# Tokens of the experts: an indirect DMA of rows and transposes on TensorE, where products with one-hot places stood

## The chip, the cores and the metric

The kernel runs on one core of a Trainium2 chip. The metric is the device time of one execution in microseconds (us). The engines are named as in the profile: PE (TensorE), DVE (VectorE), ACT (ScalarE), POOL (GpSimd), SP (SyncE, which here only issues transfers), and the 16 DMA engines of the core. Weights lie in DRAM and are streamed through on-chip memory.

## The reference, cut to what matters

512 tokens of 1024 features pass two layers (a mixer, a mixture of experts, a gated embedding) and a closing attention block. The change is in the mixture of experts. Each token goes to two of 32 experts; an expert is three matrices of 1024 x 512 floats.

```python
def hier_moe(x, w_rg, b_rg, w_re, b_re, w_gate, w_up, w_down):
    ...
    top_p, top_i = lax.top_k(pe, TOP_K)
    ...
    def expert_block(args):
        idx, e = args
        xb = x_pad[idx]
        hb = jax.nn.silu(xb @ w_gate[e]) * (xb @ w_up[e])
        return hb @ w_down[e]

    y_blocks = lax.map(expert_block, (tok_pad.reshape(n_blocks, ROUTE_BLOCK), block_expert))
    contrib = y_blocks.reshape(-1, d) * w_pad[:, None].astype(x.dtype)
    y = jnp.zeros((n + 1, d), x.dtype).at[tok_pad].add(contrib)
    return y[:n].reshape(bsz, s, d)
```

The line at issue is `xb = x_pad[idx]`: the rows of the tokens that an expert has been given. They reach the expert multiplied by the norm's gain; the norm's factor per token is put on later, with the token's weight.

## The kernel before, in words

An expert has 64 places (CAP). Two experts make a pair of 128 places, i = 0 to 15; two pairs make a batch b of four experts. Activations are kept with features on partitions: hT holds 8 blocks of 128 features by 512 tokens.

Weights come through a ring of slots of 1 MB (class Ring). SP issues a load (line 112) as soon as a slot is free; the order is a fixed plan, for each pair four quarters of g (gate), four of u (up), four of d (down), so 12 loads per pair and 192 per layer. A slot is given back when PE has used its last product. Loads that have a slot go out ahead of the branch on the overflow (line 671, `tc.If`), the others behind it.

Class Moe does a layer in this order.

- `open` and `chunk`, while the mixer's output is still being made: each block of hT is turned to tokens on partitions (tile ptok) and kept in two parts, th (the part that PE's faster float32 form holds) and tl (the rest). The last block's tl is subtracted on POOL in the route (line 539).
- `route`: the choice of experts, each token's rank among its expert's tokens, the weights in three bf16 parts (wb). On PE `embed` (pemb, line 923) fills the time. POOL does small operations on the weights (lines 598 to 654).
- `overflow`: if an expert has more than 64 tokens, a branch (line 671) does the rest. All engines pass this branch. With these inputs nothing is done in it.
- `onehot(b)`: DVE makes gt, a matrix of tokens by 256 places with a one where a token sits.
- `gather(b)`: xe, the tokens of four experts with features on partitions, as the product of th and tl with gt: 8 blocks of features x 4 blocks of tokens x 2 parts = 64 products (lines 770 and 771), the sums taken out of PSUM with the gain by ACT (773) or DVE (775). For b = 0 it is interleaved with the first g; the others stand behind d of the pair before.
- `experts`, for each pair: g and u (line 817, tiles pg, pu), silu (855) and the product hb (858), the pair before's result spread over the tokens (`combine`, pcomb, line 834, and its addition to hT on DVE, line 835), hb transposed (863) and copied (865), gt transposed for the scatter (788), the places' weights (800, four products per pair), d (881), and the result scaled into two parts (902, 903). PSUM tiles with the tag ptr, two of them, are shared by gather, transposes, scatter and weights.

What decides when something runs is the order of the code on each engine, and the semaphores between engines.

Of the kernel before, what the change touches and what calls it, by code (L numbers as in the profile page):

```python
# [13 lines left out]
I32 = mybir.dt.int32  # L14
# [11 lines left out]
EXTRA = 3  # L26

# [107 lines left out]
def body(ctx: ExitStack, tc: tile.TileContext, io, out):  # L135
# [15 lines left out]
    st_mc, mcpool = sbuf("mc", "right")  # L151
    st_keep, kpool = sbuf("keep", "left")
# [92 lines left out]
    G.iota(slots, pattern=[[1, CAP]], base=1, channel_multiplier=0, allow_small_or_imprecise_dtypes=True)  # L245

# [250 lines left out]
    class Moe:  # L497
# [3 lines left out]
        def open(self):  # L501

            l = self.l
            self.st_t, tp = sbuf(f"moe_t{l}", self.side)
            self.th = tp.tile([P, NT, D], F32R, name="th")
            self.tl = tp.tile([P, NT, D], F32R, name="tl")
# [10 lines left out]
        def chunk(self, c):  # L517
# [18 lines left out]
            def low():  # L536
                x = self.pool.tile([P, DE], F32, name="x", tag="hb").rearrange("p (t d) -> p t d", t=NT)
                A.activation(x, pt, AF.Copy)
                G.tensor_sub(self.tl[:, :, s], x, self.th.bitcast(F32)[:, :, s])
            if last:  # L540
                self.low = low
                return
            yield
            V.tensor_sub(self.tl[:, :, s], pt, self.th.bitcast(F32)[:, :, s])
# [6 lines left out]
        def route(self):  # L551
# [3 lines left out]
            ring.pump()  # L555
# [68 lines left out]
            self.low()  # L624
# [8 lines left out]
            self.onehot(0)  # L633
            V.tensor_copy(self.cnt, pr[:, NT, :])
# [22 lines left out]
            if l == 0:  # L657
                self.st_f, fpool = sbuf("further0", "left")
                ring.open(fpool, places(1), (0, "pleg", 0))
                ring.pump()  # L660

        def overflow(self):
# [8 lines left out]
            with tc.If(most > CAP), ExitStack() as st:  # L671
# [4 lines left out]
                wt = like("xe", [P, 4, DE])  # L676
                xe = wt[:, 2].rearrange("p (k s) -> p k s", s=CAP)
                gy = self.g[0].rearrange("p t e s -> p (t e s)").rearrange("p (x n) -> p x n", x=4)
                g = gy[:, 0].rearrange("p (t s) -> p t s", t=NT)
# [9 lines left out]
                with tc.For_i(0, NE // 2, 1) as i:  # L689
                    for s in range(2):  # L690
# [5 lines left out]
                        with tc.For_i(CAP, many, CAP):  # L696
                            V.tensor_scalar(base, base, float(CAP), None, op0=OP.add)
                            V.tensor_tensor(g, rk[:, :, None].to_broadcast([P, NT, CAP]),
# [57 lines left out]
        def onehot(self, b):  # L756

            self.g[b] = gt = self.pool.tile([P, NT, 4, CAP], F32R, name="gt", tag="gt", bufs=1)
            for t in (0, 2) if b == 0 else (0,):
                self.fill(gt, b, slice(t, t + 2 if b == 0 else NT))  # L760
# [1309 lines left out]
```

## Time and profile before

| | before |
|---|---|
| median of 3 runs | 1929.05 us (1926.85 to 1929.19) |
| the profiled execution | 1929.98 us |
| its span in the trace | 1928.0 us |
| PE busy | 1830.9 us, 95% |
| DVE busy | 920.6 us, 48% |
| ACT busy | 599.8 us, 31% |
| POOL busy | 292.8 us, 15% |
| DMA traffic | 477.42 MB, mean 248 GB/s |
| gather on PE (lines 770, 771), busy | 127.1 + 123.8 us, 1024 products |

The profiled execution took 1.9 us more than its span. Busy time of PE counts overlapping matmuls with their own lengths, so the sum of a group can be longer than the time in which it ran; the chain of waits gives the latter. The share of the DMA engines is a mean over the whole span, while the rate is near 420 GB/s in the two expert stages and far lower elsewhere. A product of g, u or d leaves two records on PE in the trace: a pair's g is 16 products and 32 records.

### The profile page before, as it was taken

What the parts mean: (1) busy time and instruction counts of PE and PEld (TensorE: products, weight loads), DVE (VectorE), ACT (ScalarE), POOL (GpSimd) and SP (SyncE); (2) the same over time, 40 slices, a digit from 0 to 9 for tenths busy, and PEclk for the clock granted to TensorE, in tenths of its full rate; (3) what the DMA queues carried; (4) which work ended last, traced back from release to release, by engine and by line L of the source; (5) the groups of instructions that cost most, each with busy time, mean ns of one, the idle gap of its engine ahead of it and who ended that gap; (6) DMA issues with size and microseconds to landing.
All of it is one profiled execution on the core that took longest, in us unless ns stands there. A gap on an engine that the chain in (4) does not pass through costs nothing. (4 is left out here: it accounts for less than half of the span.)

```text
span 1928.0 us, 23560 instructions
## 1 busy us (share of the span) xinstructions
PE 1830.9 (95%) x9499; PEld 1152.6 (60%) x9504; DVE 920.6 (48%) x1435; ACT 599.8 (31%) x1110; POOL 292.8 (15%) x235
## 2 busy tenths in 40 slices
PE   9999799999999999978898999999999999989999
PEld 7887444454444547856663544445444676988667
DVE  5554222332322347899731223223232656998764
ACT  5324211211111136455341111111111544446761
POOL 0000100000000022545201000000000443662013
PEclk9999899999999999998898999999999999999999
DMA  8222499999999951121446999999999123311001
GB/s 354 99 88 87 173 393 405 419 421 419 422 421 421 405 201 66 66 87 66 192 154 270 404 416 420 420 421 421 419 421 368 60 85 110 132 66 66 1 1 44
DMA packets 69001, 477.42 MB, mean 248 GB/s; under 512 B 8080, under 2 KB 9040, under 8 KB 11792
## 3 DMA queue, kind: packets, MB, share of 16 engines
q1 hardware_dynamic: 67824, 475.01, 61.5%
q8 instruction: 78, 1.28, 0.3%
q10 hardware_dynamic: 960, 0.49, 0.1%
q14 instruction: 43, 0.35, 0.1%
q0 software_dynamic: 96, 0.30, 0.0%
HBM read 473.67 MB, written 2.10 MB: 247 GB/s over the span
## 5 line engine op out<-in xcount | busy, mean ns | idle before, releaser
L350 POOL TENSOR_TENSOR wunit<-wring,wunit 128x1024 fp32r<-128x1024 f32 x61 | 151.7, 2488 | 1110.4 <-ACT wunit L349 1054.9
L817 PE MATMUL pg<-wring,xe 128*64 128x512 f32 x1024 | 231.8, 601 | 16.9 <-DVE xe L775 16.9
L881 PE MATMUL pd<-wring,hbt 128*64 128x512 f32 x1024 | 226.8, 595 | 7.8 <-issue 5.4
L817 PE MATMUL pu<-wring,xe 128*64 128x512 f32 x1024 | 225.3, 592 | 0.0
L858 DVE SCALAR_TENSOR_TENSOR hb<-pu,ws,hb 128x512 f32<-128x512 f32 x32 | 24.0, 751 | 376.1 <-PE pu L817 376.1
L881 PEld LDWEIGHTS pd<-wring,hbt 128*64 128x64 f32 x1024 | 77.7, 137 | 141.9 <-issue 127.2
L835 DVE TENSOR_TENSOR hT<-hT,pcomb 128x1024 f32<-128x1024 f32 (+1 forms) x136 | 153.1, 1154 | 17.6 <-PE pcomb L834 17.6
L817 PEld LDWEIGHTS pg<-wring,xe 128*64 128x64 f32 x1024 | 71.4, 138 | 149.6 <-issue 122.6
L817 PEld LDWEIGHTS pu<-wring,xe 128*64 128x64 f32 x1024 | 73.4, 137 | 145.1 <-issue 137.3
L834 PE MATMUL pcomb<-sc,y 128*128 128x512 f32 x512 | 143.2, 415 | 1.9 <-DVE y L903 1.3
L903 DVE SCALAR_TENSOR_TENSOR y<-pd,ws,y 128x1024 fp32r<-128x1024 f32 (+1 forms) x34 | 41.5, 1221 | 212.9 <-ACT y L902 212.9
L349 ACT ACTIVATE wunit<-wring 128x1024 fp32r<-128x1024 f32 x91 | 95.8, 1055 | 137.7 <-PE pa L259 43.4
L770 PE MATMUL pgat<-gt,th 128*128 128x256 f32 x512 | 127.1, 289 | 2.4 <-ACTq L671 2.4
L771 PE MATMUL pgat<-gt,tl 128*128 128x256 f32 x512 | 123.8, 282 | 0.0
L834 PEld LDWEIGHTS pcomb<-sc,y 128*128 128x128 f32 x512 | 88.6, 189 | 49.1 <-issue 25.6
L770 PEld LDWEIGHTS pgat<-gt,th 128*128 128x128 f32 x512 | 97.4, 190 | 28.0 <-issue 23.9
L350 DVE TENSOR_TENSOR wunit<-wring,wunit 128x1024 fp32r<-128x1024 f32 x54 | 74.2, 1376 | 66.5 <-ACT wunit L349 65.8
L902 ACT ACTIVATE y<-pd,ws 128x1024 fp32r<-128x1024 f32 (+1 forms) x34 | 36.2, 1064 | 218.1 <-PE pd L881 216.5
L865 ACT ACTIVATE hbt<-ptr 128x512 f32<-128x512 f32 x32 | 19.2, 599 | 270.3 <-PE ptr L863 270.3
L771 PEld LDWEIGHTS pgat<-gt,tl 128*128 128x128 f32 x512 | 97.6, 191 | 0.0
L257 PE MATMUL pa<-xah,wunit 128*128 128x512 f32 x192 | 77.0, 401 | 1.4 <-ACT xah L253 1.4
L855 ACT ACTIVATE hb<-pg,ws 128x512 f32<-128x512 f32 x32 | 22.0, 687 | 179.4 <-PE pg L817 179.4
(453 smaller groups left out, 3539.6 us busy)
## 6 DMA issues: line engine op xcount, KB each, us to landing
wring<-in_w_exp_gate_dram SPq DMA_DIRECT2D x128, 1024.0 KB, 10.0
wring<-in_w_exp_up_dram SPq DMA_DIRECT2D x128, 1024.0 KB, 11.0
wring<-in_w_exp_down_dram SPq DMA_DIRECT2D x128, 1024.0 KB, 11.6
wring<-in_w_in_a_dram SPq DMA_DIRECT2D x11, 1024.0 KB, 16.8
wring<-in_w_ple_gate_dram SPq DMA_DIRECT2D x8, 1024.0 KB, 5.6
wring<-in_w_in_b_dram SPq DMA_DIRECT2D x8, 1024.0 KB, 4.7
wring<-in_w_in_dram SPq DMA_DIRECT2D x8, 1024.0 KB, 4.9
wring<-in_w_out_a_dram SPq DMA_DIRECT2D x4, 1024.0 KB, 7.4
```

The costliest lines, as they stand in the source:

```text
L257: PE.matmul(ps, lhsT=wh, rhs=xh, start=first, stop=False)
L349: A.activation(h, src, AF.Copy)
L350: (eng or self.eng).tensor_sub(l, src, h.bitcast(F32))
L770: PE.matmul(pg, lhsT=self.th[:, t, s], rhs=gt[:, t, :], start=t == 0, stop=False)
L771: PE.matmul(pg, lhsT=self.tl[:, t, s], rhs=gt[:, t, :], start=False, stop=t == NT - 1)
L817: PE.matmul(pp[s * 64:(s + 1) * 64, :], lhsT=xe[:, k, c0:c0 + CAP], rhs=ring.get((self.l, i, nm, q), 2 * s + kk), start=k == 0, stop=k == ...
L834: PE.matmul(pc[:, c - c0], lhsT=ys[x][:, z, k // len(ys), :], rhs=sc, start=z == 0, stop=z == 1)
L835: V.tensor_add(hT[:, c0:c0 + n, :], hT[:, c0:c0 + n, :], pc)
L858: V.scalar_tensor_tensor(hb, pu, rsl, hb, op0=OP.mult, op1=OP.mult)
L881: PE.matmul(pd[s * 64:(s + 1) * 64, n, :], lhsT=hbt[:, j, s * CAP:(s + 1) * CAP], rhs=ring.get((l, i, "d", j), 2 * s + n), start=j == 0, s ...
L902: A.activation(yh, pc, AF.Copy, scale=w)
L903: V.scalar_tensor_tensor(yl, pc, w, yh.bitcast(F32), op0=OP.mult, op1=OP.subtract)
```

## The change

The gather's products are gone. In their place:

- `chunk` keeps the tokens whole (tile xt, plain float32) and, after four blocks each, writes them to DRAM (xd, 512 rows of 4 KB), four DMAs of 256 KB on ACT's queue.
- `indices`: for the two pairs of a batch, eight products of gt with a two-column table of token numbers (tokb), and two DVE operations give each of 256 places its token's number (tile at). An empty place gets 512, beyond the bound.
- `fetch(i)`: POOL issues an indirect DMA that reads, for each of a pair's 128 places, the row of xd with that number into tile xr[i % 2]; a place beyond the bound is passed over, and its row keeps what it held (zeros at first, put there by POOL in the route).
- `turn(i)`: eight transposes of xr on PE, in two halves of four through a ptr tile, taken out with the gain by ACT (for pair 0 by ACT and DVE in turn) into xe.
- Order: the fetches for pairs 0 and 1 stand in the route, behind onehot(0); those for pairs i + 2 and i + 3 in pair i, i even; onehot(b + 1) at the head of the even pair. A turn's two halves stand in the pair before its own, between u and d. gt is bf16 with two buffers in place of one.
- Slots: two (layer 0) or three (layer 1) early slots from `open` (EARLY = (2, 3)), and two further ones in place of one. th and tl are gone.
- In the overflow's branch, which does nothing here, the tokens come from xd as well.

```diff
@@ chunk
             if not last:
-                A.activation(self.th[:, :, s], pt, AF.Copy)
+                A.activation(self.xt[:, :, s], pt, AF.Copy)
...
             if last:
                 self.start()
-                A.activation(self.th[:, :, s], pt, AF.Copy)
...
+                V.tensor_copy(self.xt[:, :, s], pt)
+            if c % 4 == 3:
+                s = slice((c - 3) * P, (c + 1) * P)
+                for t in range(NT):
+                    nc.scalar.dma_start(out=self.xd[t * P:(t + 1) * P, s], in_=self.xt[:, t, s])
@@ open, route
+            self.st_early, pool = sbuf(f"early{l}", self.side)
+            ring.open(pool, places(EARLY[l]), (l, "pleg", 0))
...
+            self.xr = [self.pool.tile([P, D], F32, name=f"xr{i}") for i in range(2)]
+            for x in self.xr:
+                G.memset(x, 0.0)
...
-            self.low()
...
             self.onehot(0)
+            self.indices(0, self.pps.tile([P, T], F32, name="pidx", tag="ptok", bufs=4))
+            for i in range(2):
+                self.fetch(i)
...
+            ring.open(fpool, places(2), (l, "pleg", 0))
@@ new functions
+        def indices(self, b, pi):
+
+            for o in range(2):
+                g = self.places_of(2 * b + o)
                 for t in range(NT):
+                    PE.matmul(pi[:, 2 * o:2 * o + 2], lhsT=g[:, t, :], rhs=tokb[:, t, :],
+                              start=o == t == 0, stop=o == 1 and t == NT - 1, skip_group_check=True)
+            self.at = self.pool.tile([P, 2], I32, name="at", tag="at", bufs=2)
+            for o in range(2):
+                V.tensor_scalar(self.at[:, o:o + 1], pi[:, 2 * o:2 * o + 1], pi[:, 2 * o + 1:2 * o + 2], float(T),
+                                op0=OP.add, op1=OP.add)
+
+        def fetch(self, i):
+
+            G.indirect_dma_start(out=self.xr[i % 2], out_offset=None, in_=self.xd,
+                                 in_offset=bass.IndirectOffsetOnAxis(ap=self.at[:, i % 2:i % 2 + 1], axis=0),
+                                 bounds_check=T - 1, oob_is_err=False)
+
+        def turn(self, i):
+
+            xr = self.xr[i % 2]
+            self.xe[i] = xe = self.pool.tile([P, NK, P], F32, name="xe", tag="xe", bufs=1)
+            for h in range(0, NK, 4):
+                pt = self.ps.tile([P, T], F32, name="ptr", tag="ptr", bufs=2)
+                for k in range(4):
+                    PE.transpose(pt[:, k * P:(k + 1) * P], xr[:, (h + k) * P:(h + k + 1) * P], ident)
+                for k in range(4):
+                    x, src, g = xe[:, h + k, :], pt[:, k * P:(k + 1) * P], prmc(f"g_ffn{self.l}", h + k)
+                    if i == 0 and k % 2:
+                        V.tensor_scalar(x, src, g, None, op0=OP.mult)
+                    else:
+                        A.activation(x, src, AF.Copy, scale=g)
                 yield
@@ experts
+            for _ in self.turn(0):
+                pass
             for i in range(NE // 2):
                 b, o = divmod(i, 2)
-                if i:
-                    pg = self.project(i, "g")
-                else:
-                    pg = self.project(i, "g", self.gather(0))
+                more = o == 0 and b + 1 < NE // 4
+                if more:
+                    self.onehot(b + 1)
+                pg = self.project(i, "g")
+                if i == 0:
                     self.weights(0)
...
+                turn = self.turn(i + 1) if i + 1 < NE // 2 else iter(())
                 next(comb, None)
+                next(turn, None)
                 next(comb, None)
...
                 A.activation(hbt.rearrange("p j s -> p (j s)"), pt, AF.Copy)
+                for _ in turn:
+                    pass
+                next(comb, None)
+                if more:
+                    self.indices(b + 1, self.ps.tile([P, T], F32, name="pidx", tag="ptr", bufs=2))
+                    for x in range(i + 2, i + 4):
+                        self.fetch(x)
+                if i + 1 < NE // 2:
+                    self.weights(i + 1)
                 copy = self.scatter(i)
...
-                if o == 1 and b + 1 < NE // 4:
-                    for _ in self.gather(b + 1):
-                        pass
-                    if b + 2 == NE // 4:
-                        self.st_t.close()
-                    self.weights(i + 1)
```

SP's queue ahead of layer 0's branch on the overflow (the load of `most` is its first instruction). Before:

```order
L112 DMA wring<-in_w_ple_dram 128x2048
L112 DMA wring<-in_w_exp_gate_dram 128x2048 x4
L112 DMA wring<-in_w_exp_up_dram 128x2048 x4
L112 DMA wring<-in_w_exp_down_dram 128x2048 x4
L112 DMA wring<-in_w_exp_gate_dram 128x2048 x3
L665 TENSOR_LOAD most
```

The same place after:

```order
L113 DMA wring<-in_w_ple_dram 128x2048
L113 DMA wring<-in_w_exp_gate_dram 128x2048 x4
L113 DMA wring<-in_w_exp_up_dram 128x2048 x4
L113 DMA wring<-in_w_exp_down_dram 128x2048 x4
L113 DMA wring<-in_w_exp_gate_dram 128x2048 x4
L113 DMA wring<-in_w_exp_up_dram 128x2048 x2
L679 TENSOR_LOAD most
```

18 expert loads stand ahead of the branch, 15 before; in layer 1 the last gate row before is x2, so 14, and after it is again 18.

POOL's queue in layer 0's route, where the small operations on the weights (o, w) end in the casts to wb. Before:

```order
L620 TENSOR_TENSOR w_1463<-w_1463,gs 128x4
L539 TENSOR_TENSOR tl<-x,th 128x4x128
L626 TENSOR_TENSOR o_1519<-o_1474,o_1509 128x32
L637 TENSOR_TENSOR w_1530<-d,w_1463 128x4
L638 TENSOR_TENSOR o_1509<-o_1509,w_1463 128x32
```

After:

```order
L632 TENSOR_TENSOR w_1488<-w_1488,gs 128x4
L637 TENSOR_TENSOR o_1541<-o_1499,o_1534 128x32
L775 DMA xr_1427<-xd_1041,at 128x1024
L775 DMA xr_1428<-xd_1041,at 128x1024
L651 TENSOR_TENSOR w_1570<-d,w_1488 128x4
L652 TENSOR_TENSOR o_1534<-o_1534,w_1488 128x32
```

The two fetches (xr from xd by the numbers in at) stand ahead of the rest of the weights, and the subtraction for tl is gone.

PE in an odd pair of layer 0, from g to the next batch. Before, with d and the start of the gather:

```order
L817 MATMUL pg<-wring,xe 64x512 x16
L817 MATMUL pu<-wring,xe 64x512 x16
L834 MATMUL pcomb<-sc,y 128x512 x8
L863 MATMUL ptr<-ident,hb 128x128 x4
...
L834 MATMUL pcomb<-sc,y 128x512 x8
L881 MATMUL pd<-wring,hbt 64x512 x16
L770 MATMUL pgat<-gt,th 128x256
L771 MATMUL pgat<-gt,tl 128x256
```

After (xr_1427 and xr_1428 are the two tiles of rows; lines 830, 847, 881 and 903 are the old 817, 834, 863 and 881):

```order
L830 MATMUL pg<-wring,xe 64x512 x16
L830 MATMUL pu<-wring,xe 64x512 x16
L847 MATMUL pcomb<-sc,y 128x512 x4
L786 MATMUL ptr<-ident,xr_1427 128x128 x4
L847 MATMUL pcomb<-sc,y 128x512 x4
L881 MATMUL ptr<-ident,hb 128x128 x4
L786 MATMUL ptr<-ident,xr_1427 128x128 x4
L847 MATMUL pcomb<-sc,y 128x512 x4
...
L847 MATMUL pcomb<-sc,y 128x512 x4
L903 MATMUL pd<-wring,hbt 64x512 x16
L830 MATMUL pg<-wring,xe 64x512 x16
```

d is followed at once by the next pair's g, and the two half turns of the next pair stand among the combine's products.

## Rows read from the trace of the kernel before

**Rows 1.** The page, part 2: GB/s in each of 40 slices.

```profile
GB/s 354 99 88 87 173 393 405 419 421 419 422 421 421 405 201 66 66 87 66 192 154 270 404 416 420 420 421 421 419 421 368 60 85 110 132 66 66 1 1 44
```

**Rows 2.** Windows in both expert stages (window and length, busy us, PEclk, DMA share, GB/s).

```profile
440.00:640.00 200.00, 198.11 (x1035) 95.71 (x1030) 57.79 (x73) 28.00 (x43) 0.00 (x0) 1.00 1.01 421
1090.00:1450.00 360.00, 356.92 (x1876) 175.12 (x1876) 102.00 (x135) 50.39 (x79) 0.00 (x0) 1.00 1.01 418
```

**Rows 3.** The chain of waits, a batch of layer 1: start us, us, engine, tile, line.

```profile
1149.81 7.02 PE pg L817 x32
...
1194.68 7.09 PE pd L881 x32
1209.72 7.02 PE pg L817 x32
```

**Rows 4.** Waits of SP's queue in that batch: us in total, times, longest.

```profile
SPq L112 <- PE pg L817: 18.6, 8, 9.4
```

**Rows 5.** Layer 1's last expert load (a line's view: ns, first and last start).

```profile
L112 SPq DMA_DIRECT2D wring<-in_w_exp_down_dram x1: 328/328/328, 1478.9 to 1478.9; - x1
...
DMA to landing us min/median/max: 7.5/7.5/7.5
```

**Rows 6.** Line 881 on PE, layer 0, then layer 1.

```profile
L881 PE MATMUL pd<-wring,hbt x512: 592/592/643, 254.2 to 705.0; 128*64 128x512 f32 x171
...
L881 PE MATMUL pd<-wring,hbt x512: 592/592/643, 1048.9 to 1500.8; 128*64 128x512 f32 x171
```

**Rows 7.** PE by line and shape in that batch: count | busy us, mean ns | idle.

```profile
L770 PE MATMUL pgat<-gt,th 128*128 128x256 f32 x32 | 7.8, 283 | 0.0
L771 PE MATMUL pgat<-gt,tl 128*128 128x256 f32 x32 | 7.7, 284 | 0.0
L863 PE MATMUL ptr<-ident,hb 128*128 128x128 f32 x8 | 1.3, 281 | 0.0
...
L800 PE MATMUL ptr<-wb,gt 128*128 128x9 bf16 x9 | 0.7, 171 | 0.0
```

**Rows 8.** ACT by line and shape, whole span.

```profile
L531 ACT ACTIVATE junk<-ptok 128x128 f32<-128x128 f32 x64 | 17.7, 276 | 10.3 <-PE ptok L524 8.7
```

**Rows 9.** Timeline of a pair between u and d: start us, us.

```profile
1166.26 1.17 PE L834 MATMUL pcomb<-sc,y 128*128 128x512 f32 x4
```

**Rows 10.** DMA queues from 3.9 to 12 us: packets, MB, share of 16 engines.

```profile
q1 hardware_dynamic: 1337, 2.79, 95.9%
q0 software_dynamic: 48, 0.15, 4.6%
```

**Rows 11.** The first expert load of layer 1 behind the branch (a line's view).

```profile
L112 SPq DMA_DIRECT2D wring<-in_w_exp_gate_dram x1: 338/338/338, 1027.4 to 1027.4; - x1
...
DMA to landing us min/median/max: 4.8/4.8/4.8
```

**Rows 12.** Timeline of layer 1's route and first g: start us, us, engine, line.

```profile
1008.67 1.45 PE L923 MATMUL pemb<-wring 128*128 128x512 f32 x3
...
1012.79 0.20 POOL L637 TENSOR_TENSOR w<-d,w 128x4 f32<-128x4 f32 x1
...
1017.23 0.46 POOL L652 CAST wb<-left 128x192 bf16<-128x192 f32 x1
1020.93 1.28 ACT L773 ACT_TABLE_LOAD   x1 [9.69 <-DMA wg<-in_w_router_dram]
1020.98 0.48 DVE L775 TENSOR_SCALAR xe<-pgat,prm 128x256 f32<-128x256 f32 x1 [14.13 <-DMA wg<-in_w_router_dram]
...
1021.52 1.97 PE L817 MATMUL pg<-wring,xe 128*64 128x512 f32 x4 [8.00 <-DVE xe L775]
```

**Rows 13.** Tile wg: its loads on POOL.

```profile
L510 POOL DMA_DIRECT2D wg<-in_w_router_dram x2: 582/644/706, 1.8 to 941.1; - x2
```

**Rows 14.** Tile xe on DVE, layer 0: ns, first and last start.

```profile
L775 DVE TENSOR_SCALAR xe<-pgat,prm x25: 483/483/484, 226.9 to 652.6; 128x256 f32<-128x256 f32 x25
```

More of the change, by code (lines that the diff above doesn't have):

```diff
@@ L26 @@
 EXTRA = 3
+EARLY = (2, 3)
 PRM = {}
@@ L656, in route @@
             self.st_w.close()
[L657 to L660, printed above, removed]
+            self.st_t.close()
+            self.st_f, fpool = sbuf(f"further{l}", "left")
+            ring.open(fpool, places(2), (l, "pleg", 0))
+            ring.pump()
         def overflow(self):
@@ L739, in overflow @@
-                                PE.matmul(pa, lhsT=yh, rhs=sc, start=True, stop=False)
-                                PE.matmul(pa, lhsT=yl, rhs=sc, start=False, stop=True)
-                                V.tensor_add(hT[:, c, :], hT[:, c, :], pa)
-                self.fill(self.g[0], 0, slice(0, NT))
-        def places(self):
-            if self.l == 1:
-                self.st_f, fpool = sbuf("further1", "right")
-                ring.open(fpool, places(1), (1, "pleg", 0))
-            lend(self.l)
@@ L751, in fill @@
-        def fill(self, gt, b, ts):
-            n = ts.stop - ts.start
-            V.tensor_tensor(gt[:, ts], self.rank[:, ts, 4 * b:4 * b + 4, None].to_broadcast([P, n, 4, CAP]),
-                            slots[:, None, None, :].to_broadcast([P, n, 4, CAP]), op=OP.is_equal)
-        def onehot(self, b):
-            self.g[b] = gt = self.pool.tile([P, NT, 4, CAP], F32R, name="gt", tag="gt", bufs=1)
-            for t in (0, 2) if b == 0 else (0,):
-                self.fill(gt, b, slice(t, t + 2 if b == 0 else NT))
@@ L762, in gather @@
-        def gather(self, b):
-            self.xe[b] = xe = self.pool.tile([P, NK, 4 * CAP], F32, name="xe", tag="xe", bufs=1)
-            gt = self.g[b].rearrange("p t e s -> p t (e s)")
-            for k in range(NK):
-                pg = self.ps.tile([P, 4 * CAP], F32, name="pgat", tag="ptr", bufs=2)
-                s = slice(k * P, (k + 1) * P)
-                for t in range(NT):
-                    PE.matmul(pg, lhsT=self.th[:, t, s], rhs=gt[:, t, :], start=t == 0, stop=False)
-                    PE.matmul(pg, lhsT=self.tl[:, t, s], rhs=gt[:, t, :], start=False, stop=t == NT - 1)
-                if k % 2 or b and k < 2:
-                    A.activation(xe[:, k, :], pg, AF.Copy, scale=prmc(f"g_ffn{self.l}", k))
-                else:
-                    V.tensor_scalar(xe[:, k, :], pg, prmc(f"g_ffn{self.l}", k), None, op0=OP.mult)
+                                A.activation(y.rearrange("p (n m) -> p n m", n=2), pv, AF.Copy, scale=ws[:, 0:1])
@@ new lines, in overflow @@
+                                PE.matmul(pa, lhsT=y, rhs=sc.bitcast(F32), start=True, stop=True)
+                                V.tensor_add(hT[:, c, :], hT[:, c, :], pa)
+                for i in range(2):
+                    self.fetch(i)
+        def onehot(self, b):
+            self.g[b] = gt = self.pool.tile([P, NT, 4, CAP], BF16, name="gt", tag="gt", bufs=2)
+            n = 2 if b == 0 else NT
+            for t in range(0, NT, n):
+                V.tensor_tensor(gt[:, t:t + n], self.rank[:, t:t + n, 4 * b:4 * b + 4, None].to_broadcast([P, n, 4, CAP]),
+                                slots[:, None, None, :].to_broadcast([P, n, 4, CAP]), op=OP.is_equal)
@@ L1925, in body @@
     st_v.close()
-    moe.places()
     moe.route()
@@ L1931, in body @@
     moe.st_f.close()
+    moe.st_early.close()
     moe.finish(units)
@@ L1946, in body @@
     st_v.close()
-    moe.places()
     moe.route()
@@ L1953, in body @@
     moe.experts(units)
+    moe.st_f.close()
+    moe.st_early.close()
     st_extra.close()
```

77 lines of the change are left out of this document (30 added, 47 removed).

## The prediction

> **What bounds the kernel now.** I read the page's slices first: in slices 6 to 13 and 22 to 30 the DMA rate stands near 420 GB/s [rows 1]; these are the two expert stages. The windows say that inside such a stage PE and the 16 DMA engines are both full: PE 356.92 us of 360, DMA share 1.01 at 418 GB/s [rows 2], and no slice of the page does better than 422. Which of the two paces the other? The chain of waits stays on PE through a whole batch (four experts, two pairs), from g to g, 1149.81 to 1209.72, so 59.91 us [rows 3]. The waits of SP's queue agree: it waits for PE to give a slot back, 18.6 us on gate slots alone in this batch [rows 4]. So PE leads. But a load of 1.049 MB takes 2.50 us at 418 to 422 GB/s, and 24 of them 60.0: PE is first by nothing, and what is taken from it is worth only what the DMA can follow. The one cushion is the stage's end: the last expert load lands at 1478.9 + 7.5 = 1486.4 [rows 5], and PE's last d ends at 1501.4 [rows 6], 15 us later, because PE works off slots that are full.
>
> **What the change does to PE.** Removed: a batch's 64 gather products. In time that is from d's end, 1194.68 + 7.09 = 1201.77, to g at 1209.72, 7.95 us [rows 3]; their busy times, 7.8 and 7.7, overlap [rows 7]. The 7.95 hold four of the small weight products, which stay: a ninth of 0.7 each, so 0.3 us [rows 7]. Added per pair: eight transposes of 128x128. That shape is there for hb, eight in 1.3 us: 1.3 per pair [rows 7]. Added per batch: eight products of two columns for the indices; the nearest row has nine columns and 0.08 us each, 0.6 in all [rows 7]. Not shown are the hand-overs: a turn fills a PSUM buffer with four blocks, ACT empties it in four pieces of 0.276 [rows 8], 1.1 us, and its next user may wait. Nothing is the lower end; both halves uncovered is the upper, 2.2 us per pair. In the new order four comb products, 1.17 us [rows 9], and mostly more lie between a filling and the next use of its buffer, so I take 0.45, near the lower end.
> PE alone, layer 1: g starts at 1024.1 (below); the old stretch is 1501.4 - 1021.5 = 479.9; less eight gathers, 63.6; plus 15 turns of 1.75, 26.3 (the first is in the start); plus seven groups of index products, 4.2; plus the weights, 2.4. PE would end at 1473.3, and a batch is some 56 us.
>
> **What it does to the DMA.** The 24 loads stay, 60.0 us. New are the rows of two pairs: 256 places of 4 KB, 1.05 MB if all move. 512 tokens with two experts each fill 1024 of the 2048 places and the empty ones are passed over, so 0.52 MB, 1.25 us at 418 GB/s. The rows ride on another queue than the loads. That this does not make them free is seen at the kernel's start, where the loads' queue q1 holds 95.9% of the engines and q0 4.6% [rows 10]: they share one total. A batch then wants 61.3 us of DMA and 56 of PE: the DMA becomes the bound once the slots are used up. PE's lead at the start is 18 loads, since two early slots (three in layer 1) and two further ones let 18 go out ahead of the branch on the overflow where 14 did (15 in layer 0). The lead shrinks by some 5 us per batch, so it runs dry in the last two batches: PE and DMA end close together.
> The stores of the tokens (eight of 256 KB per layer) go out while the DMA has room. ACT issues them; an issue costs SP 0.34 us [rows 11], so four hold ACT 1.4, and what ACT owes POOL there is used only at 1012.79, in the tail [rows 12]: nothing.
> The Trainium skill, DMA: Bandwidth & Descriptors, section "Issuing engines are not separate DMA queues", says that DMAs of all engines end on the same 16 engines and interleave. The trace agrees, with its 95.9 + 4.6%. Were it otherwise, rival B below would be the forecast.
>
> **The stage's start, layer 1.** pemb keeps PE until 1008.67 + 1.45 = 1010.1 [rows 12]. Then index products 0.5 and two DVE steps 0.4: 1011.0. Two fetches on POOL: a direct DMA of 128 rows took POOL 0.58 to 0.71 [rows 13]; one that reads an index per row has no reason to take less than 0.65, and no bound above in the trace; I set 5 us as the end and take 1.3, twice the row. POOL goes on at 1013.6. Behind the fetches are queued POOL's tail, L637 to the last cast, 1012.79 to 1017.69, 4.9 us, and the branch, which frees DVE at 1020.98, 3.3 later [rows 12]: 1021.8, 0.8 later than now. (The subtraction for tl, ahead of the tail now, is gone.) Two half turns 0.75, ACT's table 1.28 and a piece 0.28 set g's start at 1024.1. A load's eight records cost 2 x 1.97 here [rows 12], so the first slot is free at 1028.1; today the first load goes out at 1027.4 [rows 11].
> The end by the DMA: 174 loads from 1028.1 are 435.0, seven batches of rows 8.7, and a lone load's landing, 4.8 from its issue [rows 11], adds 2.3: 1474.1. That is a quarter of d. The last quarter of u lands 10 us earlier; behind it stand its own products 1.7, comb and hb without a turn 5.2, and d 7.0, so d ends 3.9 after the last landing, at 1478.0. That is later than PE alone, so it holds: 1501.4 - 1478.0 = **23.4 us** gained.
> **Layer 0.** The first evacuation is at 226.9 now [rows 14]; + 0.8 + 6.3 gives the first free slot, 234.0; + 446.0 + 3.9 = 683.9, against 705.6 [rows 6]: **21.7 us**.
> What follows a stage (the gate, the next mixer) starts from d's end and isn't touched. The sum is 45.1. The profiled execution took 1929.98, 0.9 above the median of the runs: 1929.98 - 45.1 = 1884.9, by the median 1884. Forecast **1885**.
>
> **The rivals.**
> A, PE stays the bound: hand-overs of 1.5 us per pair in place of 0.45 put PE's end at 1473.3 + 15.8 = 1489.1; 12.3 gained in each layer, 1905. At 2.2 per pair 1.8 are left, 1926. For it: PE, ACT and two PSUM buffers are now tied in every pair. Against it: ACT is busy 50.39 us of 360 [rows 2].
> B, the rows cost the DMA nothing: the loads alone end it, 8.7 earlier; 32.1 and 30.4, 1867. PE alone, with hand-overs at nothing 1466.5, would allow it. Against it: the shares of q0 and q1 [rows 10].
> C, the fetch is dear: 5 us each at the start add 7.4 per layer, 1900; or an empty place holds an engine like a full one, and the rows cost 8.7 more per layer, 1902. For it: no row shows an indirect DMA.
> D, slower than before: a row holds its DMA engine longer than its bytes do. In a layer each engine carries 7 x 128 = 896 filled rows / 16 = 56, at 418 / 16 = 26 GB/s 0.16 us each. To use up 22.5 us per layer a row must take 0.16 + 22.5 / 56 = 0.56 us; from there the kernel loses. At 1 us it loses 24.5 per layer, 1979. For it: nothing in the trace reads scattered rows. Against it: at the start 1337 packets of 2.1 KB took 95.9% of 16 engines for 8.1 us, 0.09 us each [rows 10], so 4 KB should be 0.19 at most.
> A rule that speaks against the change is the Trainium skill, SBUF — State Buffer, section "SBUF: two separate sides": POOL cannot write the descriptors of its own DMAs while a DVE operation in a two-port mode holds the port they share. Here descriptors would come late while DVE is busy, and a turn would wait: rival E. The rows of a pair are asked for about half a batch ahead, 30 us [rows 3], and DVE is busy 102 of 360 us [rows 2], so 8 or 9 us of DVE in that time, all of it waited for, are covered. It decides only beyond 30; at 35 us of delay 5 us are lost in each of seven batches, 35 per layer, 1955.
>
> **How the numbers follow.** Forecast (1874 to 1895) 0.56, A 0.14, B 0.13, C 0.10, D 0.06, E 0.01. The likeliest gives 1885. The range, 1866 to 1910, takes in B, C and most of A, and leaves out D, E and the worse end of A. About 0.2% is what a measurement of this kernel can tell from no change. Faster by more: 0.91, all but D, E and the far end of A. Slower by more: 0.07, D and E. Within: 0.02, where A or D just eats the gain.
>
> **What would show it.** No gather on PE; batches of 56 to 57 us early in a stage and near 61 at its end; PE waiting for loads in the last pairs only, and SP there not waiting for PE; a DMA share of 1 with some 2% from q0; the last landing 4 us ahead of d's end in place of 15; 1 to 2 us of POOL per fetch; d's ends near 684 and, less what layer 0 has gained, 1478. Wrong would be turns that wait for xr (D, E), comb or d waiting for ACT in every pair (A), several us of wait ahead of the first turn (C).

## The result, and the profile of the changed kernel

The changed kernel takes 1895.99 us (median of four, 1893.39 to 1897.82), the kernel before 1929.12 in the same comparison: a ratio of 0.9829, with a 95% interval of 0.9812 to 0.9846. So 33 us were gained, of 45 forecast. The profiled execution of the changed kernel, 1893.39 us (span 1891.8), is the fastest of its four; by the two profiled executions the gain is 36.6. A second comparison of the changed kernel (five executions, median 1892.47) gave 0.9823 (0.9802 to 0.9844).

The page of the changed kernel, parts 1, 2 and 5. PE is busy for 92% of the span, where it was 95; the expert stages still stand at 420 GB/s, as in [rows 1]; and u (line 830) now waits for its weights, 25.4 us in all.

```profile
PE 1748.5 (92%) x8863; PEld 1052.0 (56%) x8864; DVE 899.2 (48%) x1421; ACT 630.2 (33%) x1276; POOL 326.4 (17%) x270
...
GB/s 361 99 91 145 228 418 420 420 420 421 421 420 419 421 291 25 87 67 67 275 171 341 421 421 420 420 420 420 420 420 377 87 96 122 103 68 68 1 1 45
...
L830 PE MATMUL pu<-wring,xe 128*64 128x512 f32 x1024 | 234.1, 597 | 25.4 <-DMA wring<-in_w_exp_up_dram 25.4
```

Line 903 (d) on PE, in layer 0 and then in layer 1. The last records start at 683.4 and 1464.5, so the last d ends at 684.0 and 1465.1, against 705.6 and 1501.4 in [rows 6].

```profile
L903 PE MATMUL pd<-wring,hbt x512: 592/592/1116, 248.0 to 683.4; 128*64 128x512 f32 x171
...
L903 PE MATMUL pd<-wring,hbt x512: 592/592/1116, 1026.9 to 1464.5; 128*64 128x512 f32 x171
```

Windows of one batch early and one late in layer 0 (busy us of PE, PEld, DVE, ACT, POOL; granted clock; DMA share; GB/s). A batch that took 59.91 us [rows 3] now takes 55.0 early in the stage, g at 256.4 to g at 311.4, with PE full; late in the stage it takes 60.6, 503.4 to 564.0, with PE busy for 55.8 of 61 (the second row), and the next one 61.3. In both the DMA is full. So the stage changes its bound on the way.

```profile
256.00:311.00 55.00, 53.66 (x275) 22.87 (x272) 16.00 (x21) 10.43 (x24) 1.99 (x2) 1.00 1.01 421
503.00:564.00 61.00, 55.82 (x276) 22.41 (x274) 16.01 (x21) 10.43 (x24) 2.00 (x2) 1.00 1.01 420
```

PE's waits (us in total, times, longest), layer 0 and then layer 1. The waits of u for its weights begin with pair 10 in layer 0 and pair 9 in layer 1; before there were none at all in this list, and SP waited for PE [rows 4].

```profile
PE pu L830 <- DMA wring<-in_w_exp_up_dram: 11.6, 22, 0.6
PE ptr L805 <- DVE at L770: 6.2, 6, 1.0
...
PE ptr L786 <- DMA xr<-xd,at: 14.8, 1, 14.8
PE pu L830 <- DMA wring<-in_w_exp_up_dram: 13.7, 25, 0.9
```

The two traces, side by side (us; the issue of the first load behind the start of g, the landing of the layer's last expert load, the end of d):

```
kernel     layer 0: first issue, last landing, d ends   layer 1: first issue, last landing, d ends
before             232.98        688.23       705.58              1027.45       1486.39      1501.35
after              231.20        679.85       683.99              1010.02       1460.87      1465.05
```

PE's end trailed the last landing by 17.4 and 15.0 us and now trails it by 4.1 and 4.2. Layer 0 gained 21.6, layer 1 a further 14.7; what stands behind layer 1's d took 426.6 and 426.7 us.

### The profile page after: what moved, and what is told of

It is laid out like the page before. It is cut to its first block, busy times and chain, and to the rows that moved or that the text cites. A ratio compares the mean times of both kernels' runs of the same rounds, so it can differ in the third digit from the quotient of the medians.

```text
span 1891.8 us, 22637 instructions
## 1 busy us (share of the span) xinstructions
PE 1748.5 (92%) x8863; PEld 1052.0 (56%) x8864; DVE 899.2 (48%) x1421; ACT 630.2 (33%) x1276; POOL 326.4 (17%) x270
## 5 line engine op out<-in xcount | busy, mean ns | idle before, releaser
L830 PE MATMUL pu<-wring,xe 128*64 128x512 f32 x1024 | 234.1, 597 | 25.4 <-DMA wring<-in_w_exp_up_dram 25.4
L848 DVE TENSOR_TENSOR hT<-hT,pcomb 128x1024 f32<-128x1024 f32 (+1 forms) x136 | 157.2, 1157 | 47.5 <-PE pcomb L847 45.9
L830 PEld LDWEIGHTS pu<-wring,xe 128*64 128x64 f32 x1024 | 68.9, 136 | 185.6 <-issue 114.9
L792 ACT ACTIVATE xe<-ptr,prm 128x128 f32<-128x128 f32 x248 | 71.2, 368 | 282.3 <-PE ptr L786 280.7
L775 POOL DMA_INDIRECT xr<-xd,at x32 | 32.2, 1006 | 721.4 <-DVE at L770 706.0
L847 PE MATMUL pcomb<-sc,y 128*128 128x512 f32 x512 | 152.6, 418 | 1.9 <-DVE y L925 1.3
L903 PEld LDWEIGHTS pd<-wring,hbt 128*64 128x64 f32 x1024 | 72.1, 138 | 140.8 <-issue 133.9
L267 PE MATMUL pa<-xah,wunit 128*128 128x512 f32 x192 | 75.5, 393 | 2.2 <-ACT xah L263 2.2
L268 PE MATMUL pa<-xal,wunit 128*128 128x512 f32 x192 | 75.5, 393 | 0.6 <-DVE xal L264 0.6
L269 PE MATMUL pa<-xah,wunit 128*128 128x512 f32 x192 | 75.3, 392 | 0.0
L1299 PE MATMUL pp<-wunit,xfh 128*128 128x256 f32 x256 | 73.6, 288 | 1.3 <-DVE wunit L360 1.3
```

The costliest lines, as they stand in the source:

```text
L267: PE.matmul(ps, lhsT=wh, rhs=xh, start=first, stop=False)
L268: PE.matmul(ps, lhsT=wh, rhs=xl, start=False, stop=False)
L269: PE.matmul(ps, lhsT=wl, rhs=xh, start=False, stop=last)
L792: A.activation(x, src, AF.Copy, scale=g)
L830: PE.matmul(pp[s * 64:(s + 1) * 64, :], lhsT=xe[:, k, s * CAP:(s + 1) * CAP], rhs=ring.get((self.l, i, nm, q), 2 * s + kk), start=k == 0, ...
L847: PE.matmul(pc[:, c - c0], lhsT=ys[x][:, z, k // len(ys), :], rhs=sc, start=z == 0, stop=z == 1)
```

## The experiments

The theory: each expert stage ends when the DMA queue has brought its last load; rows, loads and the start of the queue behind the branch add up, and PE's work doesn't show. The rival: PE, with its new transposes and hand-overs, sets the end. All times are medians; on the chip of the first four, before took 1927.73, so the changed kernel's 0.9829 is 1894.8 there.

**One fetch.** Only the rows of pairs 0 and 1 are fetched.

```diff
-                    for x in range(i + 2, i + 4):
-                        self.fetch(x)
```

> The changed kernel without the fetches inside the expert loop: only pairs 0 and 1 get their own rows, all later pairs turn the same two tiles again, so what they compute is left without its tokens. Index products, DVE steps and turns stay. Theory (the DMA queue sets the end of each expert stage, and the rows share it): seven batches of rows at some 1.25 us leave the queue in each layer, 8.7 us per layer, so 1896 - 17 = 1878 to 1879; the late batches shrink from 61.0 to 59.6 us and the early ones stay at 55.0. Rival (PE is the bound, or the rows ride beside the loads for nothing): within 2 us of 1896.

Measured: 1874.16 us, ratio 0.9727 (0.9709 to 0.9744), 20.6 less. The stretch from the first issue to the last landing is 438.0 and 439.0 us in place of 448.7 and 450.8; less 2.3 for the last landing, its 174 loads make 2.50 and 2.51 each, the price of the forecast. The stretches are 10.7 and 11.9 us shorter; 2.4 of the latter is the first load's landing, 4.8 us after its issue here and 7.2 in the changed kernel. So the rows cost 10.7 and 9.5 us per layer, not 8.7. The last batches shrank further than the 59.6 expected, to 57.7 and 57.0 us, since PE's lead now lasts into pair 12 of layer 0 and 13 of layer 1. PE's wait for u in layer 0 halves but stays, so even here the stage ends on the loads:

```profile
PE pu L830 <- DMA wring<-in_w_exp_up_dram: 5.8, 11, 0.6
```

**Empty places too.** An empty place reads token 511 and is no longer passed over.

```diff
-                V.tensor_scalar(self.at[:, o:o + 1], pi[:, 2 * o:2 * o + 1], pi[:, 2 * o + 1:2 * o + 2], float(T),
+                f = self.pool.tile([P, 1], F32, name="atf", tag="atf", bufs=2)
+                V.tensor_scalar(f, pi[:, 2 * o:2 * o + 1], pi[:, 2 * o + 1:2 * o + 2], float(T),
                                 op0=OP.add, op1=OP.add)
+                V.tensor_scalar(self.at[:, o:o + 1], f, float(T - 1), None, op0=OP.min)
```

> The changed kernel with an index of 511 for an empty place, so that it is fetched as well and not passed over: 256 rows of 4 KB per batch in place of some 128. Theory (a passed-over place costs the DMA nothing, a row its bytes): the rows cost 1.25 us more per batch, 8.7 per layer, 1913. Rival (an empty place holds an engine like a full one already): 1896. If a row costs much more than its bytes, more than 1920.

Measured: 1909.63 us, 0.9902 (0.9885 to 0.9918), 15 more than the changed kernel. The stretches are 456.7 and 456.9 us, 8.0 and 6.1 longer (7.1 in layer 1 if its first load had landed as late as in the changed kernel). Fetching an empty place costs nearly its bytes, which passing over saves (all empty places read the same row here; other rows were not tried). The DMA views of layer 0 show the changed kernel, then this one, then the kernel with one fetch (packets, MB, rate, small packets; then the queues with their share of 16 engines).

```profile
DMA packets 26878, 184.95 MB, mean 420 GB/s; under 512 B 3864, under 2 KB 3864, under 8 KB 4774
...
q1 hardware_dynamic: 24839, 180.90, 98.9%
q0 software_dynamic: 2016, 3.73, 2.3%
```

```profile
DMA packets 26938, 189.02 MB, mean 420 GB/s; under 512 B 2986, under 2 KB 2986, under 8 KB 4778
...
q0 software_dynamic: 2016, 7.34, 4.1%
```

```profile
DMA packets 24845, 181.08 MB, mean 421 GB/s; under 512 B 2758, under 2 KB 2758, under 8 KB 2758
...
q1 hardware_dynamic: 24822, 180.76, 101.1%
```

q0 holds 2.3% of the 440 us, 10.1 us, and 4.1% of 450 us, 18.5 us, when every place is fetched; the total is 420 or 421 GB/s in all three. The packets under 512 B tell what a passed-over place leaves: 3864 in the changed kernel, 2986 when none is passed over. So an empty place still puts a small packet on the queue.

**No turns.** Pairs 1 to 15 use pair 0's tokens; transposes and evacuations are left out, fetches stay.

```diff
-                turn = self.turn(i + 1) if i + 1 < NE // 2 else iter(())
+                turn = iter(())
+                self.xe[i + 1] = self.xe[i]
```

> The changed kernel without the turns of pairs 1 to 15: no transposes, no evacuations by ACT, every pair uses pair 0's tokens. Fetches and slots stay. PE loses 15 x 1.75 = 26 us of work per layer. Theory (queue): the time stays at 1896 within 4 us, the early batches go down to some 51.5 us, the late ones stay near 61, and PE's wait for loads grows by some 25 us per layer. Rival (PE and its hand-overs are the bound): 26 us less per layer, 1844.

Measured: 1895.19 us, 0.9823 (0.9805 to 0.9842): nothing gained by taking 15 turns per layer away, as the queue theory wants and the rival forbids. PE only waits longer, 23.6 us in layer 0 in place of 12.1:

```profile
PE pu L830 <- DMA wring<-in_w_exp_up_dram: 17.9, 33, 0.6
...
PE pg L830 <- DMA wring<-in_w_exp_gate_dram: 5.7, 11, 0.6
```

The early batches took 53.1 us, not the 51.5 expected: a turn costs PE 0.95 us per pair in time and not 1.75, and PE's wait grew by 11.5 us and not by 25.

**Old slots.** The number of slots of the kernel before.

```diff
-EARLY = (2, 3)
+EARLY = (0, 0)
-            ring.open(fpool, places(2), (l, "pleg", 0))
+            ring.open(fpool, places(1), (l, "pleg", 0))
```

> The changed kernel with the slots of the kernel before: no early slots and one further slot, so 15 and 14 expert loads go out ahead of the branch in place of 18 and 18. All of the computation stays. Theory (queue): three loads more are behind the stage's start in layer 0 and four in layer 1, at 2.5 us each, 17.5 us, less some 2 us since the router's weights land earlier in layer 1: 1911 to 1914. Rival (slots only smooth, they don't set the end): 1893 to 1897.

Measured: 1905.74 us, 0.9893 (0.9873 to 0.9913), 11 more, less than the 16 to 19 expected. The stretches grew as forecast, by 7.8 us for three loads and by 9.6 for four. Given back were 4.8 us in layer 1, from the first product of its residual (pres) to the last block of the tokens, where the router's weights no longer come late, and 0.9 us from there to the first turn. So the run changes two things at once; the price of a load behind the start is read from the stretches, 2.6 and 2.4 us each. In layer 0 PE waits for u 16.5 us in place of 11.6:

```profile
PE pu L830 <- DMA wring<-in_w_exp_up_dram: 16.5, 31, 0.6
```

**The kernel before with one gather.** Batches 1 to 7 use batch 0's tokens; no rows, no turns, the old slots.

```diff
-                    for _ in self.gather(b + 1):
-                        pass
+                    self.xe[b + 1] = self.xe[b]
```

> The kernel before without its gathers for batches 1 to 7 of each layer: those batches use batch 0's tokens. Nothing takes the gather's place, no rows, no turns, and the slots are those of before (15 and 14 loads ahead). PE loses 7 x 7.95 = 56 us of work per layer. Theory (queue): the loads alone set the end. Layer 1: 178 loads of 2.49 us from 1027.4, plus 2.3 for the last landing and some 4 us of PE behind it, 1477; layer 0: 177 from 233.0, 680; so 24 to 26 us per layer, 1928 - 50 = 1877 to 1881: taking the gather away for nothing is worth hardly more than the change, since 1894.8 is 33 below before on the same chip. Rival (PE's work counts in full): 112 us less, 1816.

Measured: 1893.45 us, 0.9820 (0.9805 to 0.9835). Of some 111 us of gather (14 x 7.95) that PE no longer does, 35 arrive. This is as much as the change brings, with its rows and turns: the extra slots pay for both. The expected 1877 to 1881 was too low: the stretches are 450.1 and 453.3 us where 443 and 446 were reckoned. Some 4 us of the difference are the start: the first g is still interleaved with a gather and gives its slots back slowly, so the queue runs at 270 GB/s in the ten microseconds from 1011 (a window of layer 1, columns as above, and PE's wait for u in that layer), and at 326 over the thirty behind the first issue, where the changed kernel has 383. The price of a load, 2.50 us and not 2.49, makes another 2.

```profile
1011.00:1021.00 10.00, 10.00 (x57) 4.66 (x57) 0.96 (x4) 2.92 (x4) 0.00 (x0) 1.00 0.76 270
...
PE pu L817 <- DMA wring<-in_w_exp_up_dram: 21.7, 40, 0.6
```

**Router's weights early.** wg in a place of its own, layer 1's loaded ahead of the second mixer.

```diff
+        def load(self):
+            self.wg = mcpool.tile([P, NK, 36], F32, name="wg", tag="wg")
+            G.dma_start(out=self.wg, in_=io["w_router"][:, self.l])
...
-            self.wg = self.pre.tile([P, NK, 36], F32, name="wg", tag="wg")
-            G.dma_start(out=self.wg, in_=io["w_router"][:, l])
...
+    moe1 = Moe(1, "left", pwpool)
+    moe1.load()
     mb.open()
```

> The changed kernel with the router's weights (wg) in a place of their own and layer 1's load of them issued before the second mixer, in place of 924 us, where POOL's issue waits for a DVE operation on the tile that lay there. All of the computation stays. Theory: DVE's wait of 2.0 us for wg at 931.3 goes, layer 1's route and stage start 2.3 us earlier, and since the stage's end follows its start, 2.3 us less: 1892.5 on a chip where the changed kernel takes 1894.8. Rival (the wait is covered by another one, of the chunks for the mixer's weights): no change.

Measured: 1894.03 us, 0.9822 (0.9809 to 0.9836), which cannot be told from the changed kernel's 0.9829 or 0.9823. In the trace the wait is gone and layer 1's stretch from its residual to the last block of tokens takes 62.6 us in place of 65.9; but in that execution layer 0's first g was 4 us late, 3 of them from ahead of the residual. The time leaves it open. The traces of all kernels don't: that stretch takes 65.9 to 68.4 us in the seven executions whose wg comes late and 61.1 to 63.7 (the kernel before) in the five where it doesn't, this one and the last kernel below among them.

**Rows first.** Loads that find a slot during the route are held back until behind the branch.

```diff
-        while self.loaded < len(self.plan) and (most is None or self.loaded < most):
+        while not self.hold and self.loaded < len(self.plan) and (most is None or self.loaded < most):
...
+            ring.hold = True
             self.onehot(0)
...
     moe.overflow()
+    ring.hold = False
+    ring.pump()
```

> The changed kernel with the last loads ahead of the branch (four per layer, issued in the route as slots come free) held back until behind the branch, so that the first two fetches don't share the queue with them. All of the computation stays. Theory: the second fetch of layer 1 lands some 8 us after its issue, as in layer 0, in place of 11.7; the first turn starts 3 us earlier; but four loads that went out while the queue was waiting for the stage to start now go out later. If SP issues them at once behind the branch, 1892 to 1895; if they wait until the stage starts, four loads of 2.5 us per layer come on top of the queue: 1905 to 1912. Rival (the landing of the rows doesn't hold the first turn): the first turn starts when it does now.

Measured: 1894.68 us, 0.9830 (0.9813 to 0.9846). It did not separate anything: two loads only were held, SP passed the branch early and issued them at 993.1, 1.2 us later than before, so the second fetch landed after 11.75 us again. That the loads beside it hold the fetch up rests on a comparison of layers and kernels further down, and on no run of its own.

**One tile of rows, a third further slot.** The freed 4 KB per partition pay for one slot more.

```diff
-            self.xr = [self.pool.tile([P, D], F32, name=f"xr{i}") for i in range(2)]
+            self.xr = self.pool.tile([P, D], F32, name="xr0")
...
-            ring.open(fpool, places(2), (l, "pleg", 0))
+            ring.open(fpool, places(3), (l, "pleg", 0))
...
+                if i + 2 < NE // 2:
+                    self.fetch(i + 2)
```

> The changed kernel with one tile of rows in place of two (4 KB per partition freed; pair i + 2 is fetched in pair i, right behind the turn of pair i + 1), and with the room used for a third further slot in each layer, so 19 loads ahead of the branch. All of the computation stays. Theory (queue): one load less behind each stage's start, 2.5 us per layer, 1895 - 5 = 1890, if the single tile's rows still land before their turn (asked for one pair ahead, 27 us, they take 8 to 12). Rival: the first pair's second turn waits, since its rows are asked for only when the stage starts, or the first g does; then 1895 or more.

Measured: 1888.45 us, 0.9796 (0.9781 to 0.9810), 5 to 6 less than the changed kernel and 40 less than before; its interval just overlaps that of the changed kernel's second comparison. One load less and one fetch less ahead of the first turn; no turn in the loop waits.

**The changed kernel again, and two early slots in both layers.** The last kernel is the one before it with EARLY = (2, 2) and 3 further slots in layer 0, 4 in layer 1.

> The changed kernel itself, timed beside the next one on the same chip. Both theories: 1893 to 1897, a ratio of 0.983 to before.

> The kernel with one tile of rows, with two early slots in both layers and three further slots in layer 0, four in layer 1: 19 loads ahead of the branch in each, and the router's weights of layer 1 no longer wait for the mixer's tile. All of the computation stays. Theory (queue, each stage's end follows its start): 2.5 us less in each layer from the 19th load and 2.3 to 3 us less from the router's weights, 1895 - 7.5 = 1887 to 1888; in the trace layer 1's first two blocks of the route follow each other without DVE's wait of 2.0 us. Rival (one more load beside the first rows lets them land later, and the first turn waits for them): 1890.

Measured: 1892.47 us (0.9823), just under what was expected, and 1887.26 us, 0.9785 (0.9767 to 0.9803). The last is the fastest kernel here; against the one with a single tile of rows its 1.2 us are within the intervals. In its trace layer 1's d ends at 1455.2, 9.9 us ahead of the changed kernel, of which 6.1 are left at the end of the span; where the rest goes behind the stage was not followed.

## Why the prediction was right in its way and too high in its gain

**Right: the bound and its change.** PE led by nothing, and the DMA became the bound on the way through the stage, with d's end 4.1 and 4.2 us behind the last landing (forecast 3.9). Late batches take 59.9 to 61.8 us in layer 0 and 61.0 in layer 1 (forecast 61.3). q0 holds 2.3% (forecast some 2%). Four runs put the end on the queue and not on PE: rows taken away (20.6 us less), rows doubled (15 more), loads added behind the start (11 more), turns taken away (nothing).

**Right: the PE side, a little too dear.** A batch's PE work is 55.0 us; some 56 were forecast. In the early batch from 283.27 to 338.30 the new work is this (line, engine, tile, count, busy us, mean ns, idle ahead of it):

```profile
L786 PE MATMUL ptr<-ident,xr 128*128 128x128 f32 x16 | 2.5, 279 | 0.0
...
L805 PE MATMUL ptr<-identb,gt 128*128 128x128 bf16 x8 | 0.8, 220 | 1.2 <-DVE at L770 1.0 <-ACT xe L792 0.2
L817 PE MATMUL ptr<-wb,gt 128*128 128x9 bf16 x8 | 0.5, 169 | 0.1
L766 PE MATMUL pidx<-tokb,gt 128*128 128x2 bf16 x8 | 0.4, 165 | 0.0
```

16 transposes are 2.5 us and eight index products 0.4, as read off [rows 7]. The timeline of an even pair between u and d (start, us) shows the hand-overs: only the last PSUM fill waits, 1.04 us for DVE's index steps, once per batch; 0.9 was taken for a batch.

```profile
290.14 7.04 PE L830 MATMUL pu<-wring,xe 128*64 128x512 f32 x32
...
298.14 0.60 PE L786 MATMUL ptr<-ident,xr 128*128 128x128 f32 x4
...
300.03 0.66 PE L786 MATMUL ptr<-ident,xr 128*128 128x128 f32 x4
...
303.20 0.40 PE L805 MATMUL ptr<-identb,gt 128*128 128x128 bf16 x4 [1.04 <-DVE at L770]
...
304.51 1.94 PE L903 MATMUL pd<-wring,hbt 128*64 128x512 f32 x8
```

The new work and its waits add up to some 4.4 us per batch, as forecast (2.5 + 0.4, the 1.2 ahead of L805, and 0.3 for the four weight products that stood within the gather's 7.95), but the batch grew by 3.1 only (59.91 - 7.95 = 51.96 to 55.03): part of the transposes fell into gaps that PE had in this stretch, probably those of DVE's additions for the combine. The kernel without turns says the same, 0.95 us per pair. With PE faster than forecast, its lead ran dry in pair 9 or 10 and not in the last two batches; since the queue sets the end, that cost nothing.

**Layer 0: 21.6 for 21.7, partly by luck.** The first free slot came at 231.2, not 234.0. Of these 2.8 us, 1.7 lie ahead of the change: the residual in front of layer 0 starts at 142.6 in the one execution and at 144.2 in the other (before, then after; the number behind the colon's durations is the first start).

```profile
L257 PE MATMUL pres<-vah,wunit x64: 389/389/494, 144.2 to 198.2; 128*128 128x512 f32 x64
```

```profile
L267 PE MATMUL pres<-vah,wunit x64: 389/389/502, 142.6 to 196.4; 128*128 128x512 f32 x64
```

The first turn began at 226.0, where the forecast had it once these 1.7 are taken off (226.9 + 0.8 - 1.7); the other 1.1 lie between it and the first free slot, 5.2 us and not 6.3, since ACT had loaded its table (1.28 us of the forecast's path) at 215.1, long before. Against it the stretch of the queue was 448.7 us, not 446.0: the rows' term, 8.7, was mis-sized; by the kernel with one fetch it is 10.7 (the loads alone take the other 0.7).

**Layer 1: 14.7 for 23.4.** Three terms of the sum failed.
- *"What follows a stage isn't touched"* failed. The early slots of layer 1 take the place where wg lay, so wg now lies on a tile of the mixer, and POOL's issue of its load waits for the last DVE operation on that tile (ubl, line 1207). It goes out at 924.3, 5.2 us later than before if the two traces are laid over each other at the residual's start, and behind seven expert loads where there were four. DVE then waits 1.98 us for it. Before:

```profile
952.46 0.45 DVE L521 TENSOR_TENSOR wg<-wg,prm 128x288 f32<-128x288 f32 x1
```

In the changed kernel, DVE's wait, and the issue on POOL with what it waited for:

```profile
931.30 0.46 DVE L533 TENSOR_TENSOR wg<-wg,prm 128x288 f32<-128x288 f32 x1 [1.98 <-DMA wg<-in_w_router_dram]
...
L522 POOL DMA_DIRECT2D wg<-in_w_router_dram x2: 598/672/746, 1.8 to 924.3; - x2
...
  DVE ubl L1207: 4.8, 1
```

In the kernel with two early slots the wait is gone:

```profile
927.07 0.45 DVE L533 TENSOR_TENSOR wg<-wg,prm 128x288 f32<-128x288 f32 x1
```

From the residual's first product to the last block of tokens it is 65.94 us in place of 63.65: 2.3 us.
- *The first turn's start* was mis-sized. It was reckoned from POOL's last cast and 3.3 us for the branch [rows 12]; in layer 0 it came 4.5 us behind that cast (221.56 to 226.03), in layer 1 6.9 (998.53 to 1005.44). The landing of the rows was not in the sum, and for layer 1 the profile names it as what ended PE's wait (the first pair of rows is layer 0, the second layer 1):

```profile
L775 POOL DMA_INDIRECT xr<-xd,at x2: 999/1046/1093, 214.2 to 215.6; - x2
...
DMA to landing us min/median/max: 7.7/8.2/8.6
...
L775 POOL DMA_INDIRECT xr<-xd,at x2: 998/1038/1077, 991.2 to 992.6; - x2
...
DMA to landing us min/median/max: 9.5/10.6/11.7
...
1005.44 1.94 PE L786 MATMUL ptr<-ident,xr 128*128 128x128 f32 x8 [14.76 <-DMA xr<-xd,at]
```

That name is right for a small part only. In layer 1 the second fetch, with four expert loads issued within two microseconds of it, landed at 1004.3, 11.7 us after its issue. But the larger part is POOL's way through the branch. Its queue at the branch, the kernel before in layer 1, the changed kernel in layers 0 and 1, and the kernel with one tile of rows in layer 1 (COMPARE_BRANCH is POOL's arrival, the EVENT_SEMAPHORE rows are its first five steps behind the branch; ns, first and last start), with PE's first turn in the last one:

```profile
L671 POOLq EVENT_SEMAPHORE  x5: 17/43/43, 1020.2 to 1020.6; - x5
L671 POOLq COMPARE_BRANCH  x1: 50/50/50, 1017.6 to 1017.6; - x1
...
L685 POOLq EVENT_SEMAPHORE  x5: 17/43/43, 225.1 to 225.4; - x5
L685 POOLq COMPARE_BRANCH  x1: 45/45/45, 221.6 to 221.6; - x1
...
L685 POOLq EVENT_SEMAPHORE  x5: 17/42/43, 1003.6 to 1004.5; - x5
L685 POOLq COMPARE_BRANCH  x1: 58/58/58, 998.4 to 998.4; - x1
...
L683 POOLq EVENT_SEMAPHORE  x5: 17/43/43, 1002.9 to 1003.2; - x5
L683 POOLq COMPARE_BRANCH  x1: 58/58/58, 997.7 to 997.7; - x1
...
1004.19 1.94 PE L783 MATMUL ptr<-ident,xr 128*128 128x128 f32 x8 [12.91 <-DMA xr<-xd,at]
```

POOL was through after 2.6 us before, 3.4 in layer 0 and 5.1 in layer 1. In layer 1 of the changed kernel it then waited 0.6 us for the second fetch to land (its five steps take 0.9 us, elsewhere 0.3 or 0.4). The last kernel tells the two apart: its only fetch had landed at 1001.3, 2.9 us ahead of the turn, and the profile names it all the same; POOL needed 5.1 us again, and the turn came 6.4 us after it had reached the branch, 6.9 in the changed kernel. In all kernels' traces the passage takes 2.6 to 3.4 us where one load was left from before when POOL came, 4.1 where there were two, and 5.0 to 6.0 where there were three or so, in layer 1 of nine of them. Why loads should lengthen it was not tested. 1002.1 was due for this turn (1021.8 on the old axis, less the 19.7 by which the route is earlier here); it came 3.3 us later. ACT had its table here too (since 991.8), and from the turn to the first free slot it was 4.6 us and not 6.3, so 1.6 us were lost. How long the second fetch takes goes with the loads issued just ahead of it or beside it: 7.7 us with two (layer 0), 10.5 and 9.7 with three (the kernel with old slots, layers 0 and 1), 11.7 with four.
- *The queue's term*: 450.8 us, not 446.0. The first load behind the branch landed 7.2 us after its issue and not 4.8, which makes 2.4 and was not explained; the loads alone take 1.6 more than reckoned (438.95 for 437.3 in the kernel with one fetch); the rows make 0.8 (9.5 for 8.7).

Sum: 2.3 + 1.6 + 4.8 = 8.7 us, which is what layer 1 lacks. The rest up to the medians (33.1 against 36.6) is that the profiled execution was the fastest of its four.

**The rivals.** A fell with the kernel without turns. B fell with the kernel with one fetch: the rows are paid for. The Trainium skill, DMA: Bandwidth & Descriptors, section "Issuing engines are not separate DMA queues", says that all DMAs end on the same 16 engines; the shares of q0 and q1 and the 20.6 us agree. C fell on both counts: a fetch holds POOL for 1.0 us (1.3 in the sum), and passing over an empty place saves the 8.0 and 7.1 us per layer that fetching it costs. Its sign, several microseconds of wait ahead of the first turn, did show in layer 1, where the turn came 3.3 us late, but mostly by the branch and for 0.6 us by the landing of the rows. D fell with the empty places: 10.1 us of q0 in layer 0 are some 0.18 us for each of its 900 or so rows, the small packets counted in, far below the 0.56 from which the kernel would lose. E: the rows of the loop land 7.9 to 11.4 us after their issue, their turns stand 23 us or more behind it (30 were taken), and no turn of the loop appears in PE's waits for them.

## What to carry to other kernels

When an engine and the DMA are both full in a stage, work taken off the engine is worth only what the transfers can follow: here some 111 us of products for 33 to 36. What moves the end then is the length of the queue behind the stage's start, so a buffer that lets one more load go out early is worth that load's time, 2.4 to 2.6 us here, less what its place costs, and a buffer freed elsewhere (4 KB of rows) pays at once. A new buffer also moves others: look where the small tiles behind it now lie, and what their loads have to wait for. And a wait that the profile puts down to a transfer is worth a second look at when that transfer landed.

## What the runs showed that was not expected

- A place that the indirect DMA passes over still leaves a packet of under 512 B on the queue: 3864 such packets in layer 0's window with the empty places, 2986 without them. The filled places cost the queue 10.7 and 9.5 us per layer, the empty ones, when fetched, 8.0 and 7.1 more.
- An indirect DMA for 128 places took POOL 1.0 us. With one load left on the queue it landed 4.3 us after its issue (pair 1 of layer 1 in the kernel with one tile of rows, issued at 1006.4); the second of two fetches landed after 7.7 us with two loads about it, 9.7 and 10.5 with three, and 11.7 with four.
- The granted clock fell to 0.50, the lower of its two levels (1.2 GHz), while PE stood idle ahead of each stage, and rose again among the first products of g: 10.2 us in each stage before, 13.7 in the changed kernel. The first turn's eight transposes take 1.94 us there, four in the loop 0.60 to 0.66. For g the sum had this price, in the 1.97 of [rows 12].
- The residual ahead of layer 0, which has the same code in all kernels, started between 142.5 and 145.6 us in their profiled executions; the medians of two comparisons of the same kernel lie 3.5 us apart. An edit worth 2 us can be seen in a trace here, and hardly in a time.
